# Dilated attention of a three-mixer encoder block: statistics and weights sent in other steps, the combination's small steps in PSUM, small jobs handed out every 2 products, another order at the end

## The chip, the cores and the metric

The kernel runs on one core of a Trainium2 chip. The metric is the device time of one execution in microseconds (us), as the median of several runs. One further execution was recorded by the hardware profiler; its own time and its span are given below. The core has five engines that run their own instruction streams and meet at semaphores: PE (TensorE, matmul, with weight loads shown apart as PEld), DVE (VectorE), ACT (ScalarE), POOL (GpSimd) and SP (SyncE, which here issues the DMAs, in order). Data is in SBUF (128 partitions), products come out in PSUM, which has 8 banks of 128 x 512 numbers in this kernel's use.

## The reference

One encoder block: a norm, one wide projection, three mixers side by side, a merge, an output projection, a norm and a residual. S = 1024 tokens, width D = 1024, each mixer 512 wide. The change is in the first mixer, dilated attention: 8 heads of 64, each computed in three groups (window, dilation) = (128, 1), (512, 4), (2048, 16), which are merged by a softmax over the groups' log-denominators.

```python
outs, lses = [], []
for gi, (window, dil) in enumerate(A_GROUPS):
    hs = slice(gi * A_HEADS, (gi + 1) * A_HEADS)
    o_g, lse_g = dilated_window_attention(aq[:, :, hs], ak[:, :, hs], av[:, :, hs], window, dil)
    outs.append(o_g)
    lses.append(lse_g)
wts = jax.nn.softmax(jnp.stack(lses, axis=0), axis=0)
oa = jnp.einsum('gbsh,gbshd->bshd', wts, jnp.stack(outs, axis=0)).reshape(b, s, BRANCH_WIDTH)
...
ya = (oa * jax.nn.silu(ga)) @ w_br_a
yb = (ob * jax.nn.silu(gb)) @ w_br_b
ym = (om * jax.nn.silu(gm)) @ w_br_m
merged = gates[:, :, 0] * ya + gates[:, :, 1] * yb + gates[:, :, 2] * ym
x = x + rms_norm(merged @ w_out, g_post)
```

## The kernel before

**Where the change lies.** The kernel runs its stages one after the other. In each, one or two kinds of work that use little PE are woven between long products that use nothing else, so that PE always has something to do. The last but one stage is the dilated attention, woven with the first 16 of the 24 branch projections (8 column tiles for each of 3 branches, the branch of this mixer last, since its operand is only then ready). The last stage (PSUM phase `ps_o`, function `y_part`) computes the rest of the projections and the output projection.

**Precision.** Operands of the big products are split into a high part (rounded, by ACT) and a low part (the difference, by DVE or POOL); each product is three matmuls: high x high, high x low, low x high. `wh` is the tile of a projection's split weights, `hh` and `hl` the two parts of this mixer's merged output, `bh` and `bl` those of the second mixer's.

**The products.** `add_y` queues projection m = 0 to 15: two halves of 512 tokens, each 12 matmuls (line 1880) into one of two PSUM banks `d`. What belongs to them, but isn't a matmul, is put on the list `pend`: the load of the weights of m + 2 (`y_load`, tile wr), the split of those of m + 1 (`y_split`: ACT line 1357, POOL line 1358), the load of the merge gate of m + 1 (`th_load`, tile wl), and the evacuation of each half (`y_evac`: DVE line 1378 multiplies in the bank, DVE line 1380 adds it to `acc`, which frees the bank). `weave` takes one job from `pend` after every third matmul. The products of m = 16, 17 and 18 have their weights split ahead too (17 and 18 into attention tiles that are free by then, `ak` and `aq`).

**The attention.** There are 12 items, (pair of heads p_, group g), g fastest. `plan` runs an item in four visits b and, after each, two steps T = 2b and 2b + 1 (`rest`). A visit computes scores (lines 1580, 1587), mask and exponential (1599 DVE, 1600 ACT), transposes the probabilities (1611, 1626, 1635, with DVE's copy to SBUF in 1639, tile `app`) and multiplies values with them (1652, 1659); the second half of an item overlaps with the first half of the next. `stats`, in visit 1 of the next item, transposes the minima and denominators, copies them (ACT) and writes them to `std` in DRAM (lines 1683 to 1690).

**The combination.** When all three groups of a pair are done, `ready` puts the 14 steps of `combine` on `todo`: fetch the statistics of the three groups, `shares` and `weights` (small DVE and ACT steps on 128 x 16 and 128 x 48 numbers, lines 1789 to 1803), `put` the weights to DRAM (`wgd`), `load` them spread over partitions (tile `wgt`, a ring of two), multiply the group's output (`weigh`, POOL line 1815), add (POOL line 1813), multiply with the SiLU gate (POOL line 1818, the gate itself in the `wgt` ring as well), and store or keep. `STEP_T` holds the step T of the current item in which each of the 14 is issued. Since `wgt` has two buffers, the load of group 2 waits for the multiply of group 0 and the gate's load for that of group 1.

**The last pair.** For p_ = 3 nothing is left to hide a trip through DRAM, so its weights are made otherwise: `rows` loads the statistics of groups 0 and 1 at T = 2 and T = 6 of the last item, `shares_3` turns them (line 1918) and computes weights in PSUM, `wide` (line 1952) spreads them with a matmul into banks W3B, and `first_two` and `third` (lines 1958 to 1966) combine the groups in halves of 512 tokens. `dl_high` (ACT, line 1858) and `dl_low` (line 1861) split the result, on DVE for the last pair.

**Order.** Each engine runs its instructions as issued, save that attention pieces are issued at a raised priority; `weave` moves to the next attention piece when the share of attention cost spent falls behind the share of product cost spent, so the costs given to the pieces decide where in the row of products each piece falls. DMAs go out on SP in order, those waiting for a buffer too.

Of the kernel before, what the change touches and what calls it, by code (L numbers as in the profile page):

```python
# [16 lines left out]
NT = 8  # L17
P = 128
# [32 lines left out]
def block(ctx: ExitStack, tc: tile.TileContext, x, xT, memT, cst, msk, bcst, tabA, gpost,  # L51
# [15 lines left out]
    def phase_psum(name, s2=0, s1=0, t=0, o=0):  # L67
        assert 2 * s2 + s1 + t + o <= 6
        bank["n"] = (s2, s1, t, o)
        bank["pool"] = tc.tile_pool(name=name, bufs=1, space=bass.MemoryType.PSUM, reuse_waits="tile")  # L70
        bank["p"] = bank["pool"].__enter__()
# [10 lines left out]
    def pst():  # L82
        return bank["p"].tile([P, 4, 128], F32, name="tr", tag="t", bufs=bank["n"][2])
# [90 lines left out]
    pend = []  # L174

    def weave(count, att=None, att_cost=0.0, lead=1.0, prio=ATT_PRIO):
        dg = run_items(count)
        dc = cost_items(count)
        d = a = 0.0
        steps = 0  # L180
        live_d, live_a = True, att is not None
        while live_d or live_a:
            if live_d and (not live_a or a / att_cost >= min(1.0, d / dc * lead)):
                try:
                    d += next(dg)
                    steps += 1
                    if pend and steps % 3 == 0:
                        pend.pop(0)()
                except StopIteration:
                    live_d = False  # L190
                    d = 1e18
            else:
                try:
                    with tc.high_priority(offset=prio):
                        a += next(att)
                except StopIteration:
                    live_a = False
# [1288 lines left out]
    with ExitStack():  # L1486
# [26 lines left out]
        def item(p_, g):  # L1513
# [155 lines left out]
            def stats():  # L1669
# [4 lines left out]
                if g == 0:  # L1674
                    A.activation(sr.rearrange("p (b a) -> p b a", b=16), tp[0:32, 0, :].rearrange("p (a b) -> p b a", b=16), AF.Copy)
                elif g == 1:
                    A.activation(sr.rearrange("p (b a) -> p b a", b=4), tp[0:32, 0, :].rearrange("p (a b) -> p b a", b=4), AF.Copy)
                else:
                    A.activation(sr, tp[0:32, 0, :], AF.Copy)
                dst = std[p_, g].rearrange("s h x -> (s h) x")  # L1680
# [14 lines left out]
                values=values, scores=scores, soft=soft, trans=trans, pv=pv, stats=stats)  # L1695

        def plan(it, pre, nxt):
# [7 lines left out]
            def tokens(T):  # L1705
# [11 lines left out]
                if n == 11:  # L1717
# [3 lines left out]
                    if T in (2, 6):  # L1721
                        j = T // 6
                        nc.sync.dma_start(rows[32 * j:32 * j + 32], std[3, j].rearrange("s h (t a) -> (s h t) a", t=NT))
# [5 lines left out]
            def visit(b):  # L1729
# [13 lines left out]
                if not it:  # L1743
                    shares_3(b)
                    return
# [7 lines left out]
            def rest(T):  # L1753
                combining(T)
                tokens(T)

            for b in range(4):
                out.append((lambda b=b: visit(b), SOFT + 100.0 if it else LAST_PAD))
                if it:
                    out += [(lambda T=T: rest(T), 0.5 * SOFT + 50.0) for T in (2 * b, 2 * b + 1)]  # L1760
# [9 lines left out]
        def combine(p_, ogs):  # L1770
# [15 lines left out]
            def shares():  # L1786
                cpt = c["t"]
                mn = cb.tile([P, 16], F32, name="cmn", bufs=2)
                V.tensor_tensor(mn, cpt[:, 0, 0], cpt[:, 1, 0], op=OP.min)
                V.tensor_tensor(mn, mn, cpt[:, 2, 0], op=OP.min)  # L1790
                c["e"] = eg = cb.tile([P, 3, 16], F32, name="ceg", bufs=1)
# [3 lines left out]
            def weights():  # L1795
                cpt, eg = c["t"], c["e"]
                dn = cb.tile([P, 3, 16], F32, name="cdn", bufs=1)
                V.tensor_tensor(dn, eg, cpt[:, :, 1], op=OP.mult)
                ds_ = cb.tile([P, 16], F32, name="cds", bufs=2)
                V.tensor_tensor(ds_, dn[:, 0], dn[:, 1], op=OP.add)  # L1800
                V.tensor_tensor(ds_, ds_, dn[:, 2], op=OP.add)
                V.reciprocal(ds_, ds_)
                V.scalar_tensor_tensor(eg, eg, 0.5, ds_[:, None, :].to_broadcast([P, 3, 16]), op0=OP.mult, op1=OP.mult)

            def put():
                for h in range(2):
                    E.dma_start(wgd[p_, h].rearrange("g (i e) -> i g e", e=16), c["e"][h * 64:h * 64 + 64])
# [26 lines left out]
        STEP_T = (4, 0, 1, 1, 2, 5, 6, 7, 7, 0, 3, 4, 5, 7)  # L1834
# [25 lines left out]
        def dl_low(k, t=slice(0, S)):  # L1860
            (V if k == 3 else G).tensor_tensor(hl[k][:, t], DL[k][:, t], hh[k][:, t].bitcast(F32), op=OP.subtract)
# [88 lines left out]
        def wide(g, x):  # L1950
            W3B[g, x] = pst().rearrange("p a b -> p (a b)") if g == 2 or x else pss1()
            PE.matmul(W3B[g, x], spread[:, g].rearrange("p h q -> p (h q)"), C["w"][0:96, half[x]], start=True, stop=True)

        def first_two(x):
            t = half[x]
            a, b = C["ogs"]
            for g, z in enumerate((a, b)):
                V.tensor_tensor(z[:, t], W3B[g, x], z[:, t], op=OP.mult)
            V.tensor_tensor(a[:, t], a[:, t], b[:, t], op=OP.add)

        def third(x):
            t = half[x]
            a, b = C["ogs"][0], OG[3, 2]
            V.tensor_tensor(b[:, t], W3B[2, x], b[:, t], op=OP.mult)
            V.tensor_tensor(a[:, t], a[:, t], b[:, t], op=OP.add)
            V.tensor_tensor(a[:, t], a[:, t], DL["g"][:, t], op=OP.mult)

        def ending():
# [3 lines left out]
                    (lambda: [third(0), dl_high(3, lo)], 2500.0)]  # L1972
# [8 lines left out]
        weave(16, every(), FIRST_PAD + 12 * NT * (SOFT + 100.0) + 4 * LAST_PAD + 10500.0)  # L1981
# [4 lines left out]
        third(1)  # L1986
        dl_high(3, hi)
        dl_low(3, lo)
        dl_low(3, hi)
# [344 lines left out]
```

## Time and profile before

| | us |
|---|---|
| median of 3 runs | 1414.26 |
| lowest, highest run | 1413.9, 1415.91 |
| the profiled execution | 1412.71 |
| its span, first to last instruction | 1410.9 |
| PE busy in it | 1379.7 |
| POOL busy in it | 574.7 |

The profile has a page (busy time of each engine, the chain of work that ended last, groups of instructions) and views of the trace: waits (who waited, for what, us in total, times, longest), windows (busy time of each engine in a stretch) and a timeline (start in us from the span's start, duration in us, engine, line of the kernel, operation, output<-input, shapes, and how many such instructions in a row the line stands for). A bracket at the end of a timeline row gives idle time of that engine just before and the event that ended it. In `PE d L1880 <- POOL wh L1358`, PE waited before writing d in line 1880 for POOL's writing of wh in line 1358. PE's matmuls overlap each other, so a matmul that shows 0.4 us starts well under 0.4 us after the one before.

### The profile page before, as it was taken

The numbers are of one execution on the slowest core, as the hardware profiler recorded it, in microseconds if no ns is written. First come the engines' busy times: TensorE is split into PE (matmuls) and PEld (weight loads), VectorE is DVE, ScalarE is ACT, GpSimd is POOL, SyncE is SP. The second block draws the span as 40 slices with busy tenths as digits, with TensorE's granted clock in tenths as the row PEclk, the third lists the DMA queues.
The fourth block names the chain that finished last, engine by engine and source line by source line (L and its number), as shares of the span: only waits on it lengthen the run. The fifth ranks groups of instructions, "written<-read, shape, count | busy, mean of one in ns | idle before, by whom it ended". The sixth has DMA issues, their size and how long they took to land.

```text
span 1410.9 us, 21845 instructions
## 1 busy us (share of the span) xinstructions
PE 1379.7 (98%) x7775; PEld 1106.2 (78%) x7775; DVE 1025.7 (73%) x1828; ACT 658.5 (47%) x1384; POOL 574.7 (41%) x440
## 2 busy tenths in 40 slices
PE   7999999999999999999999999999999999989997
PEld 7799986666655789988888888888887777767886
DVE  7768677767776597776877776677776557568977
ACT  6544355666555345333333333333345666653332
POOL 0507702675766000244555554455541153461003
PEclk9999999999999999999999999999999999999999
DMA  6355522322243688424332333333345676765455
GB/s 230 105 179 209 187 107 88 109 89 72 83 139 120 218 258 257 130 83 149 96 95 96 111 119 109 116 105 120 119 146 209 198 223 203 248 168 198 146 201 179
DMA packets 121933, 212.30 MB, mean 150 GB/s; under 512 B 32512, under 2 KB 61024, under 8 KB 121824
## 3 DMA queue, kind: packets, MB, share of 16 engines
q1 hardware_dynamic: 112512, 196.98, 43.0%
q10 hardware_dynamic: 9312, 13.93, 2.7%
q8 instruction: 61, 1.00, 0.3%
q14 instruction: 48, 0.39, 0.1%
HBM read 144.48 MB, written 66.38 MB: 149 GB/s over the span
## 4 chain that ended last, share of the span: by engine, by line
PE 87%; DVE 4%; POOL 3%; ACT 2%; issue 2%; DMA 1%; SPq 0%; DVEq 0%; POOLq 0%; ACTq 0%
PE s L1324 34%; PE d L1880 5%; PE s L1234 4%; PE s L2103 4%; PE ov L819 4%; PE sc L2021 3%; PE s L1285 3%; PE d L145 3%; PE d L147 3%; PE d L143 3%; PE s L1587 2%; PE s L804 2%; PE tr L1659 2%; PE s L803 2%; PE tr L785 2%
## 5 line engine op out<-in xcount | busy, mean ns | idle before, releaser
L810 POOL TENSOR_TENSOR bl<-bl,bp 128x512 f32<-128x512 f32 x96 | 132.7, 1382 | 54.2 <-ACT bp L806 48.7
L1324 PE MATMUL s<-hh,vS 128*128 128x512 f32 x400 | 133.4, 395 | 0.0
L1324 PE MATMUL s<-vA,vS 128*128 128x512 f32 x450 | 106.6, 390 | 0.0
L1599 DVE CUSTOM_DVE_ANT_0 pra<-s,mask 128x192 f32<-128x192 f32 (+2 forms) x192 | 52.7, 326 | 69.3 <-PE s L1587 34.7
L106 DVE TENSOR_TENSOR vS<-vot,vS 128x512 fp32r<-128x512 f32 x75 | 86.3, 1152 | 19.9 <-ACT vS L105 19.9
L1324 PEld LDWEIGHTS s<-vA,vS 128*128 128x128 f32 x450 | 84.5, 188 | 18.3
L806 ACT ACTIVATE bp<-s 128x512 f32<-128x512 f32 x128 | 75.6, 595 | 46.0 <-PE s L804 45.2
L786 DVE TENSOR_REDUCE bn<-tr 128x1 f32<-128x512 f32 x128 | 84.6, 683 | 11.0 <-PE tr L785 10.0
L1600 ACT ACTIVATE pra<-pra,sts 128x192 f32<-128x192 f32 (+2 forms) x176 | 75.2, 429 | 35.6 <-DVE sts L1599 35.3
L143 PE MATMUL d<-hh,wh 128*128 128x512 f32 x224 | 89.3, 399 | 1.3 <-DVE fth L216 1.3
L147 PE MATMUL d<-hh,wl 128*128 128x512 f32 x224 | 89.4, 399 | 0.0
L1324 PEld LDWEIGHTS s<-hh,vS 128*128 128x128 f32 x400 | 75.3, 188 | 17.7
L145 PE MATMUL d<-hl,wh 128*128 128x512 f32 x224 | 88.9, 397 | 0.0
L1324 PE MATMUL s<-hl,vS 128*128 128x512 f32 x200 | 79.1, 395 | 0.0
L1324 PE MATMUL s<-hh,wh 128*128 128x512 f32 x200 | 78.4, 392 | 0.0
L1324 PE MATMUL s<-hh,wl 128*128 128x512 f32 x200 | 78.4, 392 | 0.0
L1324 PE MATMUL s<-hl,wh 128*128 128x512 f32 x200 | 77.8, 389 | 0.0
L1328 ACT ACTIVATE vv<-s 128x512 f32<-128x512 f32 x50 | 29.9, 598 | 85.8 <-PE s L1324 59.2
L1068 POOL TENSOR_TENSOR vot<-wr 128x512 f32<-128x512 f32 x13 | 22.2, 1707 | 111.5 <-DVE wl L106 111.5
L819 PE MATMUL ov<-bp,VS 128*64 128x512 f32 x256 | 58.5, 598 | 0.0
L1068 POOL TENSOR_TENSOR vot<-vot,vA 128x512 f32<-128x512 f32 x12 | 19.3, 1608 | 90.8 <-DVE vS L106 90.8
L143 PEld LDWEIGHTS d<-hh,wh 128*128 128x128 f32 x224 | 42.2, 188 | 14.9 <-issue 5.5
(628 smaller groups left out, 4056.3 us busy)
## 6 DMA issues: line engine op xcount, KB each, us to landing
wr<-in_wu SPq DMA_DIRECT2D x40, 512.0 KB
vA<-in_wu SPq DMA_DIRECT2D x24, 512.0 KB
qkd<-ko SPq DMA_DIRECT2D x96, 128.0 KB
wl<-thd SPq DMA_DIRECT2D x24, 512.0 KB
wos<-os SPq DMA_DIRECT2D x12, 512.0 KB
wr<-in_wbr SPq DMA_DIRECT2D x24, 256.0 KB
aq<-qkd SPq DMA_DIRECT2D x12, 512.0 KB
ak<-qkd SPq DMA_DIRECT2D x12, 512.0 KB
```

What stands on the lines that cost most here:

```text
L106: V.tensor_tensor(dst_l, src, dst_h.bitcast(F32), op=OP.subtract)
L143: PE.matmul(dst, wh[:, k, :], hh[k][:, t], start=k == 0, stop=False)
L145: PE.matmul(dst, wh[:, k, :], hl[k][:, t], start=False, stop=False)
L147: PE.matmul(dst, wl[:, k, :], hh[k][:, t], start=False, stop=k == 7)
L786: fp["last"] = V.tensor_reduce(st[i]["n"][:, j, c:c + 1], s, axis=AX.X, op=OP.min)
L806: A.activation(pp, s, AF.Exp, scale=-1.0)
L810: G.tensor_tensor(lsum[i % 2], lsum[i % 2], pp, op=OP.add)
L819: PE.matmul(o[e * 64:e * 64 + 64], VS[:, kt, kv], d.pop(kt), start=kt < 2, stop=kt >= NT - 2)
L1234: PE.matmul(now[j], a, b, start=k == 0 and q == 0, stop=k == 3 and q == 2)
L1324: PE.matmul(BANK[n, c], a, b, start=k == 0 and q == 0 and not more, stop=k == 3 and q == 2, skip_group_check=c in "XW")
L1600: A.activation(src, src, AF.Exp, scale=-1.0, bias=bias, accum_out=sts[:, 1, h, T:T + 1])
L1880: PE.matmul(ps_, a, b, start=k == 0 and q == 0, stop=k == 3 and q == 2)
```

## The change

It has five parts.

1. The transfers of an item's statistics leave `stats` and become `send`, in step T = 3 of the next item (before: in visit 1). The second `rows` load of the last pair goes from T = 6 to T = 5.
2. `STEP_T`: most of the 14 steps of the combination are issued one step T later, `put` and the loads of groups 0 and 1 in steps of their own, and the load of group 2 in T = 0 of the next item.
3. `shares` and `weights` work in a PSUM bank: a copy and two minima, difference, exponential, product with the denominators and their sum (one reduction in place of two additions); only the reciprocal and the finished weights are in SBUF.
4. In this stage a job from `pend` is taken after every second matmul.
5. The end: `shares_3` becomes pieces of its own; `first_two` and `third` write their products back into the banks; the last half of `third` is a piece of the weave where it stood after it; the gate of the last pair and its low part go from DVE to POOL, in halves; `wide` skips banks of the ring `t` until group 2 gets the third and fourth of it; the attention's total cost in `weave` goes from 10500 to 13000 beyond the visits.

```diff
@@ -67,6 +67,7 @@
     def phase_psum(name, s2=0, s1=0, t=0, o=0):
         assert 2 * s2 + s1 + t + o <= 6
         bank["n"] = (s2, s1, t, o)
+        bank["i"] = 0
         bank["pool"] = tc.tile_pool(name=name, bufs=1, space=bass.MemoryType.PSUM, reuse_waits="tile")
         bank["p"] = bank["pool"].__enter__()
 
@@ -80,6 +81,7 @@
         return bank["p"].tile([P, 512], F32, name="s1", tag="s1", bufs=bank["n"][1])
 
     def pst():
+        bank["i"] += 1
         return bank["p"].tile([P, 4, 128], F32, name="tr", tag="t", bufs=bank["n"][2])
 
     def pso():
@@ -171,7 +173,7 @@
     def cost_items(count):
         return sum(q[2] for q in queue[done[0]:done[0] + count])
 
-    pend = []
+    pend, pace = [], [3]
 
     def weave(count, att=None, att_cost=0.0, lead=1.0, prio=ATT_PRIO):
         dg = run_items(count)
@@ -184,7 +186,7 @@
                 try:
                     d += next(dg)
                     steps += 1
-                    if pend and steps % 3 == 0:
+                    if pend and steps % pace[0] == 0:
                         pend.pop(0)()
                 except StopIteration:
                     live_d = False
@@ -1677,6 +1679,10 @@
                     A.activation(sr.rearrange("p (b a) -> p b a", b=4), tp[0:32, 0, :].rearrange("p (a b) -> p b a", b=4), AF.Copy)
                 else:
                     A.activation(sr, tp[0:32, 0, :], AF.Copy)
+                d["sr"] = sr
+
+            def send():
+                sr = d["sr"]
                 dst = std[p_, g].rearrange("s h x -> (s h) x")
                 if g == 0:
                     for z in range(4):
@@ -1692,7 +1698,7 @@
             return dict(
                 key=(p_, g),
                 ahead=seq[p_ * 3 + g + 2] if p_ * 3 + g + 2 < len(seq) else None,
-                values=values, scores=scores, soft=soft, trans=trans, pv=pv, stats=stats)
+                values=values, scores=scores, soft=soft, trans=trans, pv=pv, stats=stats, send=send)
 
         def plan(it, pre, nxt):
 
@@ -1718,8 +1724,8 @@
                     if T == 6:
                         DL["g"] = cb.tile([P, S], F32, name="wgt", bufs=2)
                         nc.sync.dma_start(DL["g"], g2d[0, 3])
-                    if T in (2, 6):
-                        j = T // 6
+                    if T in (2, 5):
+                        j = T // 5
                         nc.sync.dma_start(rows[32 * j:32 * j + 32], std[3, j].rearrange("s h (t a) -> (s h t) a", t=NT))
 
             def ready():
@@ -1741,7 +1747,6 @@
                 if b == 1 and pre and it:
                     pre["stats"]()
                 if not it:
-                    shares_3(b)
                     return
                 if b in (0, 2):
                     it["values"](b // 2)
@@ -1751,12 +1756,16 @@
                     qk_fetch(*it["ahead"])
 
             def rest(T):
+                if T == 3 and pre:
+                    pre["send"]()
                 combining(T)
                 tokens(T)
 
             for b in range(4):
-                out.append((lambda b=b: visit(b), SOFT + 100.0 if it else LAST_PAD))
-                if it:
+                out.append((lambda b=b: visit(b), SOFT + 100.0 if it else 0.5 * LAST_PAD))
+                if not it:
+                    out.append((lambda b=b: shares_3(b), 0.5 * LAST_PAD))
+                else:
                     out += [(lambda T=T: rest(T), 0.5 * SOFT + 50.0) for T in (2 * b, 2 * b + 1)]
             return out
 
@@ -1785,26 +1794,28 @@
 
             def shares():
                 cpt = c["t"]
-                mn = cb.tile([P, 16], F32, name="cmn", bufs=2)
-                V.tensor_tensor(mn, cpt[:, 0, 0], cpt[:, 1, 0], op=OP.min)
-                V.tensor_tensor(mn, mn, cpt[:, 2, 0], op=OP.min)
-                c["e"] = eg = cb.tile([P, 3, 16], F32, name="ceg", bufs=1)
+                b = pst().rearrange("p a b -> p (a b)")
+                mn = b[:, 0:16]
+                c["e"] = eg = b[:, 16:64].rearrange("p (g x) -> p g x", g=3)
+                c["n"] = b[:, 64:112].rearrange("p (g x) -> p g x", g=3)
+                V.tensor_copy(mn, cpt[:, 0, 0])
+                for g in (1, 2):
+                    V.tensor_tensor(mn, mn, cpt[:, g, 0], op=OP.min)
                 V.tensor_tensor(eg, cpt[:, :, 0], mn[:, None, :].to_broadcast([P, 3, 16]), op=OP.subtract)
                 A.activation(eg, eg, AF.Exp, scale=-1.0)
 
             def weights():
-                cpt, eg = c["t"], c["e"]
-                dn = cb.tile([P, 3, 16], F32, name="cdn", bufs=1)
+                cpt, eg, dn = c["t"], c["e"], c["n"]
                 V.tensor_tensor(dn, eg, cpt[:, :, 1], op=OP.mult)
                 ds_ = cb.tile([P, 16], F32, name="cds", bufs=2)
-                V.tensor_tensor(ds_, dn[:, 0], dn[:, 1], op=OP.add)
-                V.tensor_tensor(ds_, ds_, dn[:, 2], op=OP.add)
+                V.tensor_reduce(ds_, dn.rearrange("p g x -> p x g"), axis=AX.X, op=OP.add)
                 V.reciprocal(ds_, ds_)
-                V.scalar_tensor_tensor(eg, eg, 0.5, ds_[:, None, :].to_broadcast([P, 3, 16]), op0=OP.mult, op1=OP.mult)
+                c["w"] = w = cb.tile([P, 3, 16], F32, name="ceg", bufs=1)
+                V.scalar_tensor_tensor(w, eg, 0.5, ds_[:, None, :].to_broadcast([P, 3, 16]), op0=OP.mult, op1=OP.mult)
 
             def put():
                 for h in range(2):
-                    E.dma_start(wgd[p_, h].rearrange("g (i e) -> i g e", e=16), c["e"][h * 64:h * 64 + 64])
+                    E.dma_start(wgd[p_, h].rearrange("g (i e) -> i g e", e=16), c["w"][h * 64:h * 64 + 64])
 
             def weigh(g, add=False):
                 wv = wgt[g].rearrange("p (b a) -> p a b", b=16)
@@ -1831,7 +1842,7 @@
                     lambda: weigh(1, True), lambda: load(2), load_gate, lambda: weigh(2), lambda: weigh(2, True), gate, store]
 
         todo = []
-        STEP_T = (4, 0, 1, 1, 2, 5, 6, 7, 7, 0, 3, 4, 5, 7)
+        STEP_T = (5, 0, 1, 2, 3, 6, 7, 0, 0, 1, 4, 5, 6, 7)
         seq = [(p_, g) for p_ in range(4) for g in range(3)]
         items = [item(*x) for x in seq] + [None]
 
@@ -1858,7 +1869,7 @@
             A.activation(hh[k][:, t], DL[k][:, t], AF.Copy)
 
         def dl_low(k, t=slice(0, S)):
-            (V if k == 3 else G).tensor_tensor(hl[k][:, t], DL[k][:, t], hh[k][:, t].bitcast(F32), op=OP.subtract)
+            G.tensor_tensor(hl[k][:, t], DL[k][:, t], hh[k][:, t].bitcast(F32), op=OP.subtract)
 
         def add_y(m):
             n, i, f = steps[m]
@@ -1948,28 +1959,32 @@
                 dl_low(2)
 
         def wide(g, x):
+            while g == 2 and bank["i"] % 4 != 2 + x:
+                pst()
             W3B[g, x] = pst().rearrange("p a b -> p (a b)") if g == 2 or x else pss1()
             PE.matmul(W3B[g, x], spread[:, g].rearrange("p h q -> p (h q)"), C["w"][0:96, half[x]], start=True, stop=True)
 
         def first_two(x):
             t = half[x]
             a, b = C["ogs"]
-            for g, z in enumerate((a, b)):
-                V.tensor_tensor(z[:, t], W3B[g, x], z[:, t], op=OP.mult)
-            V.tensor_tensor(a[:, t], a[:, t], b[:, t], op=OP.add)
+            V.tensor_tensor(W3B[0, x], W3B[0, x], a[:, t], op=OP.mult)
+            V.tensor_tensor(a[:, t], W3B[1, x], b[:, t], op=OP.mult)
+            V.tensor_tensor(a[:, t], W3B[0, x], a[:, t], op=OP.add)
 
         def third(x):
             t = half[x]
             a, b = C["ogs"][0], OG[3, 2]
-            V.tensor_tensor(b[:, t], W3B[2, x], b[:, t], op=OP.mult)
-            V.tensor_tensor(a[:, t], a[:, t], b[:, t], op=OP.add)
-            V.tensor_tensor(a[:, t], a[:, t], DL["g"][:, t], op=OP.mult)
+            V.tensor_tensor(W3B[2, x], W3B[2, x], b[:, t], op=OP.mult)
+            V.tensor_tensor(a[:, t], W3B[2, x], a[:, t], op=OP.add)
+            G.tensor_tensor(a[:, t], a[:, t], DL["g"][:, t], op=OP.mult)
+            dl_high(3, t)
+            dl_low(3, t)
 
         def ending():
             DL[3] = C["ogs"][0]
             return [(lambda: [wide(g, 0) for g in range(2)], 500.0), (lambda: [wide(g, 1) for g in range(2)], 500.0),
                     (lambda: [first_two(0), wide(2, 0)], 2500.0), (lambda: [first_two(1), wide(2, 1)], 2500.0),
-                    (lambda: [third(0), dl_high(3, lo)], 2500.0)]
+                    (lambda: third(0), 2500.0), (lambda: third(1), 2500.0)]
 
         def every():
             yield from first()
@@ -1978,15 +1993,12 @@
             yield from run(plan(None, items[-2], None))
             yield from run(ending())
 
-        weave(16, every(), FIRST_PAD + 12 * NT * (SOFT + 100.0) + 4 * LAST_PAD + 10500.0)
+        pace[0] = 2
+        weave(16, every(), FIRST_PAD + 12 * NT * (SOFT + 100.0) + 4 * LAST_PAD + 13000.0)
         while pend:
             pend.pop(0)()
         y_split(18, V, qk.tile([P, S], R, name="aq", bufs=2))
         y_load(19)
-        third(1)
-        dl_high(3, hi)
-        dl_low(3, lo)
-        dl_low(3, hi)
         out_pool()
         for nm in ("B11", "B21"):
             for k in range(4):
```

## The prediction

> **What bounds the kernel now.** I read the page first: engines, then the chain by engine.
>
> ```profile
> span 1410.9 us, 21845 instructions
> PE 1379.7 (98%) x7775; PEld 1106.2 (78%) x7775; DVE 1025.7 (73%) x1828; ACT 658.5 (47%) x1384; POOL 574.7 (41%) x440
> PE 87%; DVE 4%; POOL 3%; ACT 2%; issue 2%; DMA 1%; SPq 0%; DVEq 0%; POOLq 0%; ACTq 0%
> ```
>
> TensorE is busy 98% of the span and carries 87% of the chain. The diff neither adds nor removes a product, so only stalls of PE in the edited stage (1065 to 1286 us) can be won or lost. That sends me to the waits, PE alone, in that window (us in total, times, longest):
>
> ```profile
> PE sc L2021 <- DVE og L1964: 2.7, 1, 2.7
> PE d L1880 <- DMA wgt<-wgd: 2.2, 1, 2.2
> PE tr L1659 <- DVE app L1639: 1.7, 1, 1.7
> ...
> ```
>
> Single stalls, each from another cause; with three shorter ones, shown below, they are a to f in order of time. A view of windows of pure products gives the unit: 46 in 10 us, a pitch of 0.22 us; a stall costs the distance of two starts less 0.22. The columns are busy us (and instructions) of PE, PEld, DVE, ACT, POOL, then granted clock, DMA share, GB/s; the first three rows are used later.
>
> ```profile
> 1154.00:1156.00 2.00, 2.00 (x34) 1.73 (x32) 0.20 (x1) 0.02 (x1) 2.00 (x2) 1.00 1.09 290
> 1204.00:1206.00 2.00, 2.00 (x30) 2.00 (x28) 0.00 (x0) 0.00 (x0) 1.54 (x1) 0.66 1.09 303
> 1206.00:1208.00 2.00, 2.00 (x25) 1.50 (x22) 0.64 (x9) 1.40 (x4) 1.92 (x2) 0.50 0.90 304
> 1310.00:1320.00 10.00, 10.00 (x46) 8.27 (x45) 9.38 (x13) 5.48 (x11) 0.00 (x0) 1.00 0.41 126
> ```
>
> The rest comes from the timeline: start, duration, engine, work, and in brackets idle time and its releaser.
>
> **The change part by part.** *Stalls a and b, the small halves of the weights (`y_split` on POOL, tile wh) behind a combining step.*
>
> ```profile
> 1157.51 0.40 PE L1880 MATMUL d<-hl,wh 128*128 128x512 f32 x1
> 1158.16 0.73 PE L1880 MATMUL d<-hh,wh 128*128 128x512 f32 x2 [0.25 <-POOL wh L1358]
> ...
> 1193.70 5.85 POOL L1815 TENSOR_TENSOR og<-og,wgt 128x1024 f32<-128x1024 f32 x2 [15.49 <-DMA wgt<-wgd]
> 1199.62 2.38 POOL L1813 TENSOR_TENSOR og<-og 128x1024 f32<-128x1024 f32 x1
> 1200.72 0.40 PE L1880 MATMUL d<-bl,wh 128*128 128x512 f32 x1
> 1201.96 1.26 POOL L1358 TENSOR_TENSOR wh<-wr,wh 128x512 fp32r<-128x512 f32 x1
> 1203.28 0.51 PE L1880 MATMUL d<-bh,wh 128*128 128x512 f32 x1 [2.15 <-DMA wgt<-wgd]
> ```
>
> The waits view names a DMA for b, but PE started 0.06 us after POOL's split ended (1201.96 + 1.26): POOL did two multiplies and an add in a row and the split stood behind the add. Pace 2 (the deferred small jobs handed out every 2 products in place of 3) and the shifted steps put both splits ahead of that 2.38 us add. Each becomes 2.38 us early against waits of 0.65 - 0.22 = 0.4 (a) and 2.56 - 0.22 = 2.3 (b): both go. After b the granted clock was 0.66 and 0.50 in two windows of 2 us, worth 0.34 x 2 + 0.50 x 2 = 1.7 more. a and b: 0.4 + 2.3 + 1.7 = 4.4.
>
> [...]
>
> *Stall c, the small steps of `combine`.*
>
> ```profile
> 1183.90 0.21 DVE L1803 SCALAR_TENSOR_TENSOR ceg<-ceg,cds 128x48 f32<-128x48 f32 x1
> ...
> 1234.33 2.38 POOL L1861 TENSOR_TENSOR hl<-hl,hh 128x1024 fp32r<-128x1024 f32 x1 [8.77 <-DMA avp<-vdr]
> 1234.39 2.38 DVE L1803 SCALAR_TENSOR_TENSOR ceg<-ceg,cds 128x48 f32<-128x48 f32 x1
> 1235.77 1.09 PE L1659 MATMUL tr<-app,avs 128*64 128x128 f32 x16
> 1238.54 0.90 PE L1659 MATMUL tr<-app,avs 128*64 128x128 f32 x12 [1.68 <-DVE app L1639]
> ```
>
> The same 128x48 instruction took 0.21 us once and 2.38 us here, where it began 0.06 us behind a POOL instruction and ended with it. Both its inputs lay in SBUF; PE then waited 1.7 us for the copy of probabilities queued behind it. In the changed kernel one input of each such step is in PSUM, so I price it at 0.21. But at this place pace 2 puts the two instructions of one evacuation (0.68 each, the L1380 row below) ahead of and inside the chain; about half of that is beyond the slack, so 0.65 of the wait stays. Gain 1.7 - 0.65 = 1.05 (bounds: 0.3 if both instructions count whole, 1.7 if none).
>
> *Stall d, evacuation of y products.*
>
> ```profile
> 1249.86 0.40 PE L1880 MATMUL d<-bh,wh 128*128 128x512 f32 x1
> 1250.37 0.68 DVE L1380 TENSOR_TENSOR acc<-d,acc 128x512 f32<-128x512 f32 x1
> 1251.20 0.47 PE L1880 MATMUL d<-bh,wh 128*128 128x512 f32 x1 [0.95 <-DVE acc L1380]
> ```
>
> PE waited for a bank whose add was popped too late: 1.34 - 0.22 = 1.1. Two evacuations of two halves handed out every 2 products instead of 3 come, by the order of the two programs, some 6 products (1.3 us) sooner; d goes whole.
>
> *Stall e, statistics of the last pair.*
>
> ```profile
> 1259.75 0.38 SPq L1723 DMA_DIRECT2D rows<-std  x1
> ...
> 1262.73 0.44 PE L1611 MATMUL tr<-cs,pra 128*128 128x128 f32 x2
> 1264.18 0.24 PE L1918 MATMUL s<-cs,rows 64*128 64x64 f32 x1 [1.01 <-issue]
> ```
>
> L1918 needs the second `rows` load, issued after the wl and g2d transfers; it is the only thing ready for PE. In the changed kernel it is issued at T=5, ahead of both, so sooner by the time that issuing them takes, and its packets don't follow 512 KB of theirs. 1.45 us between the starts less the second small transpose: 1.2 gained (bounds 0.5, 1.2). `send`, the std transfers one step later, delays nothing on this path: fetch waits for the last group's, and STEP_T moves fetch from T=4 to T=5 with it.
>
> *Stall f, the end.*
>
> ```profile
> 1281.41 0.39 PE L2021 MATMUL sc<-hh,wh 128*128 128x512 f32 x1
> 1283.10 0.68 DVE L1358 TENSOR_TENSOR aq<-wr,aq 128x512 fp32r<-128x512 f32 x1
> 1283.69 0.69 DVE L1964 TENSOR_TENSOR og<-tr,og 128x512 f32<-128x512 f32 x1
> 1284.52 0.47 PE L2021 MATMUL sc<-hh,ak 128*128 128x512 f32 x1 [2.72 <-DVE og L1964]
> ```
>
> The product pair m=17 takes the bank that `third(1)` (L1964) was reading, and this stood after 4 evacuation instructions and a split on DVE: 3.11 - 0.22 = 2.9. The change puts `third(1)` into the weave, aligns the bank so that m=17 needs only `first_two(1)` (about 2 us ahead of PE in my walk through the new order), and m=18 `third(1)`. It goes whole. The new price: the gates and small halves go to POOL in halves (1.26 each, the L1358 row above), and the split of aq waits, on ACT behind hh and on DVE beside POOL's last half. Walking the order with these durations, aq ends 0.9 us after PE needs it for its third product. Bounds 0 and 2.5 (two POOL halves in front).
>
> [...]
>
> *Load(2) after the next item's value loads.*
>
> ```profile
> 1149.98 1.26 SPq L1779 DMA_DIRECT2D wgt<-wgd  x2
> 1151.34 1.82 SPq L1529 DMA_DIRECT2D avs<-vdr  x2
> ...
> 1159.62 2.92 POOL L1815 TENSOR_TENSOR og<-og,wgt 128x1024 f32<-128x1024 f32 x1 [1.52 <-DMA wgt<-wgd]
> ...
> 1169.75 1.27 POOL L1358 TENSOR_TENSOR wh<-wr,wh 128x512 fp32r<-128x512 f32 x1
> 1171.47 0.39 PE L1880 MATMUL d<-bl,wh 128*128 128x512 f32 x1
> ```
>
> This is the one part that can lose much. POOL works in order, and the third multiply waited for this load (1159.62 - 1149.98 = 9.6 us from issue); the next split of the weights stands 11.4 us of POOL work behind it and finished 0.45 us before PE used it. Now load(2) comes on SP behind avs (1.82 us of issuing) and wl (512 KB, which the first window above moves in 1.8 us at 290 GB/s), which used to come after it. I take 2.0 later, between either alone and both (3.6): the split ends at 1173.0, PE needs it at 1171.5 - 0.4 (stall a gone) + 1.0 (pairs of products fall some 4 products later beside the attention) = 1172.1. Cost 1.0, bounds 0 and 2.6 (load 3.6 later), with the 1.7 of clock possible on top. At pair 1 the same chain has 4 us in hand:
>
> ```profile
> 1212.46 1.27 POOL L1358 TENSOR_TENSOR wh<-wr,wh 128x512 fp32r<-128x512 f32 x1 [0.20 <-ACT wh L1357]
> 1217.75 0.40 PE L1880 MATMUL d<-bl,wh 128*128 128x512 f32 x1
> ```
>
> *At nothing:* the other steps of `combine`, each one T later: POOL's wait for load(0), 15.49 us above, is empty time with nothing behind it that PE uses soon, and the results go to operands read after the weave. `send`: the same transfers, and SP no longer stands before sr when the queue has other loads to issue (a gain of which I count nothing). copy, reduction and exponential in PSUM (one DVE instruction fewer for each pair; about 0.2 us each, as L1803 above, and covered by products at all places but c); `shares_3` as pieces of its own (same work, same DVE queue).
>
> **Sum.** Gains 4.4 + 1.05 + 1.1 + 1.2 + 2.9 = 10.65; costs 1.0 + 0.9 = 1.9; net 8.75. The profiled execution took 1412.71 us (span 1410.9 and 1.8 around it): 1404.0 for it. The median of the runs, 1414.26, is 1.55 above that execution, so 1405.5 beside the median.
>
> **The rivals.**
> 1. *Half of it.* Load(2) comes 4 to 5 us later, the chain on POOL stalls PE at pair 0 (4.5 - 1.0 = 3.5 and 1.7 of clock) and c stays whole (1.05): net 10.65 - 1.05 - 0.9 - 5.2 = 3.5, so 1410.8. For it: POOL already waited 1.52 for that load with DMA share at 1.09. Against: avs and wl together are under 3 us of that rate.
> 2. *Slower.* Load(2) comes X late and stops both pairs' chains: (X - 1.0) at pair 0, (X - 4.0) at pair 1, and twice 1.7 of clock, against 10.65 - 0.9 = 9.75. From X = 5.7 the kernel isn't faster, from 7.1 it is slower by over 0.2%; at X = 8 it is 1414.26 - 9.75 + 4 + 7 + 3.4 = 1418.9. For it: 15.49 us of POOL's waiting on the earlier load. Against: the load would take 17.6 us where it took 9.6.
> 3. *It doesn't do what it says.* The stalls were not from the queues I name but from whatever is last behind them: an earlier split waits for its own load (wr), a bank freed earlier waits for its weights. Then each 2 us removed comes back at the next product: 1414.3. Against: in b, d and f the releaser ended within 0.15 us of PE's start.
>
> **How the numbers follow.** Forecast 0.62, rival 1 0.18, rival 3 0.08, rival 2 0.12. About 0.2% (2.8 us) is what a measurement of this kernel can tell from no change: faster means under 1411.4, slower over 1417.1. Faster: 0.62 and, of rival 1, 0.14: 0.76. Slower: 0.11 of rival 2. Within: 0.13. The forecast's own bounds: gains from 9.2 (c and e low) to 11.3, costs from 0 to 6.8: 1403 to 1411.9. The range runs from 1401, for queues that give more than I walked through, to 1412.5, where rival 1's upper half ends.
>
> **What would show it.** Right: no wait of PE over 0.7 us at wh, acc, rows or og; granted clock at 1.00 from 1200 to 1210; every L1803 at about 0.2 us (its successor in PSUM); m=17 starting straight behind m=16. Wrong: a new wait of PE for wh near 1172 or 1217, with POOL idle before its third multiply on wgt<-wgd; a wait for aq over 2.5 us near 1285; a low granted clock after either.

## The result and the profile after

| | us |
|---|---|
| before, median of 6 runs (lowest, highest) | 1414.43 (1413.9, 1415.91) |
| changed, median of 6 runs (lowest, highest) | 1408.0 (1406.78, 1410.23) |
| ratio to before, 95% interval | 0.9954 (0.9941 to 0.9967) |
| changed, the profiled execution (span) | 1409.11 (1407.3) |

The changed kernel is 6.4 us faster where 8.8 were forecast (1414.26 to 1405.5). Its waits of PE in the stage, read as before (us in total, times, longest):

```profile
PE d L1891 <- POOL wh L1360: 3.8, 1, 3.8
PE sc L2033 <- DVE aq L1360: 0.7, 1, 0.7
PE tr L1661 <- DVE app L1641: 0.3, 1, 0.3
PE tr L1654 <- DVE app L1615: 0.2, 1, 0.2
```

Line numbers have moved: 1891 is the product that was 1880, 1360 the split that was 1358. None of the six waits of before is left at its old size: no acc, no rows, no og, and the copy behind the small steps is down from 1.7 to 0.3. One wait is new and larger than any before. The timeline around it, from the load of group 2 for pair 0 on:

```profile
1148.79 2.57 SPq L1531 DMA_DIRECT2D avs<-vdr  x2
...
1151.45 0.57 SPq L1367 DMA_DIRECT2D wl<-thd  x1
...
1152.12 1.10 SPq L1788 DMA_DIRECT2D wgt<-wgd  x2
...
1163.55 2.94 POOL L1826 TENSOR_TENSOR og<-og,wgt 128x1024 f32<-128x1024 f32 x1 [6.90 <-DMA wgt<-wgd]
...
1170.75 0.40 PE L1891 MATMUL d<-bl,wh 128*128 128x512 f32 x1
...
1173.65 1.27 POOL L1360 TENSOR_TENSOR wh<-wr,wh 128x512 fp32r<-128x512 f32 x1
...
1174.97 0.80 PE L1891 MATMUL d<-bh,wh 128*128 128x512 f32 x1 [3.82 <-POOL wh L1360]
```

SP issues the two value loads and wl, and only then wgt. The multiply on POOL waits 6.90 us for it (1.52 before), and the split of the weights of m = 8, which needs nothing of this load, stands behind it in POOL's queue. PE starts 0.05 us after the split ends. Windows of 2 us over the same place (busy us and instructions of PE, PEld, DVE, ACT, POOL; granted clock, DMA share, GB/s) show what the gap leaves behind:

```profile
1172.00:1174.00 2.00, 0.00 (x0) 0.00 (x0) 0.10 (x1) 0.00 (x0) 2.00 (x2) 0.80 0.91 285
1174.00:1176.00 2.00, 1.03 (x3) 0.59 (x5) 0.00 (x0) 0.00 (x0) 0.92 (x1) 0.50 0.91 295
1176.00:1178.00 2.00, 2.00 (x12) 1.71 (x11) 0.30 (x1) 0.00 (x0) 0.00 (x0) 0.50 0.78 215
1178.00:1180.00 2.00, 2.00 (x10) 1.90 (x9) 1.62 (x9) 1.83 (x7) 0.00 (x0) 0.50 0.12 12
```

At a granted clock of 0.50, PE is busy for 1.03 + 2.00 + 2.00 us: half of that, 2.5 us, is lost besides the 3.8. The six waits of before make 8.7 us, and 1.7 of clock: 10.4. Those of the changed kernel make 5.0 and 2.5: 7.5. The difference, 2.9, accounts for most of the 3.6 us between the two profiled spans (1410.9 and 1407.3). The medians lie further apart than these two executions: that of before took 1.7 us less than its median, that of the changed kernel 1.1 more than its own.

Of all runs behind the numbers in this document one is left out: 1942.57 us, of the kernel with the second load of rows at T = 6, with a mean granted clock of 0.655 where all others have 0.99 to 1.00.

### The profile page after: what moved, and what is told of

It reads as the page before. It is cut to its first block, busy times and chain, and to the rows that moved or that the text cites. A ratio compares the mean times of both kernels' runs of the same rounds, so it can differ in the third digit from the quotient of the medians.

```text
span 1407.3 us, 21847 instructions
## 1 busy us (share of the span) xinstructions
PE 1381.3 (98%) x7775; PEld 1108.0 (79%) x7775; DVE 1021.6 (73%) x1824; ACT 658.8 (47%) x1384; POOL 579.7 (41%) x444
## 4 chain that ended last, share of the span: by engine, by line
PE 88%; DVE 3%; POOL 2%; ACT 2%; DMA 2%; issue 1%; SPq 0%; DVEq 0%; POOLq 0%; ACTq 0%
PE s L1326 34%; PE d L1891 6%; PE s L1236 4%; PE s L2115 4%; PE ov L821 3%; PE d L147 3%; PE d L145 3%; PE d L149 3%; PE s L1287 3%; PE sc L2033 3%; PE s L1589 2%; PE tr L1661 2%; PE s L806 2%; PE s L805 2%; PE tr L787 2%; PE d L2115 2%
```

## The experiments

The kernels ran in three groups, each beside the kernel before on the same chip. Its medians there were 1413.74, 1414.92 and 1414.08, so a distance between medians of two groups is good to about 1.2 us; ratios are free of that. "T7" is the changed kernel with load(2) at T=7.

| kernel | median us | ratio to before | 95% interval |
|---|---|---|---|
| changed, again | 1407.41 | 0.9954 | 0.9938 to 0.997 |
| changed, load(2) at T=7 ("T7") | 1402.9 | 0.9923 | 0.9911 to 0.9936 |
| T7, again | 1402.61 | 0.9916 | 0.9898 to 0.9935 |
| changed, split of m = 8 on DVE | 1404.64 | 0.993 | 0.9913 to 0.9948 |
| changed, pace 3 | 1409.13 | 0.9971 | 0.9961 to 0.998 |
| changed, small steps in SBUF | 1411.21 | 0.9978 | 0.9967 to 0.9989 |
| changed, old end | 1407.05 | 0.9954 | 0.9938 to 0.997 |
| T7, old end | 1408.94 | 0.9963 | 0.9949 to 0.9977 |
| T7, pace 3 | 1409.89 | 0.9969 | 0.9958 to 0.998 |
| T7, rows at T=6 | 1407.95 | 0.9958 | 0.9944 to 0.9971 |
| T7, statistics sent in visit 1 | 1409.7 | 0.9973 | 0.9953 to 0.9993 |
| before, pace 2 alone | 1408.8 | 0.9966 | 0.9952 to 0.998 |

### Load(2) back at T=7

```diff
-lambda: weigh(1, True), lambda: load(2), load_gate,
+lambda: load(2), lambda: weigh(1, True), load_gate,
-STEP_T = (5, 0, 1, 2, 3, 6, 7, 0, 0, 1, 4, 5, 6, 7)
+STEP_T = (5, 0, 1, 2, 3, 6, 7, 7, 0, 1, 4, 5, 6, 7)
```

> The changed kernel with one step moved back: load(2) is issued at T=7, ahead of the next item's value loads, as before the change; nothing else differs, POOL's order is the same. In the changed kernel's profile the third multiply waited 6.90 us for that load and PE then waited 3.82 us for wh at 1171 us, with the granted clock at 0.50 until 1180 (2.5 us more). Theory (the place of load(2) costs the stall and the low clock behind it): both go, 6.3 us, median 1401.7 where the changed kernel has 1408.0, no wait of PE for wh. Rival (the DMA engines are full there and the load lands as late from either place, or the value loads pay for it): the third multiply starts within 1 us of where it did, or a wait for app or avs of 3 us takes its place; median 1407 to 1409.

The timeline has the load issued 3.6 us sooner and the multiply without any wait; the waits of PE in the stage are all that is left.

```profile
1148.53 1.10 SPq L1788 DMA_DIRECT2D wgt<-wgd  x2
...
1157.28 2.94 POOL L1826 TENSOR_TENSOR og<-og,wgt 128x1024 f32<-128x1024 f32 x1
```

```profile
PE sc L2033 <- DVE aq L1360: 0.7, 1, 0.7
PE tr L1661 <- DVE app L1641: 0.3, 1, 0.3
PE tr L1654 <- DMA avs<-vdr: 0.2, 1, 0.2
```

The multiply starts 6.3 us sooner, the wait for wh is gone, the granted clock is 1.00 in every window of 1 us from 1064 to 1296, and the value loads, now behind wgt, cost 0.2. The median of 1402.9 is 5.1 below the changed kernel's 1408.0 (1.2 short of the theory). The same file a second time:

> The kernel with load(2) at T=7 once more, beside the changed kernel. Theory: 5 to 6.3 us below the changed kernel, ratio to before 0.991 to 0.9935, no low clock anywhere in the stage. Rival (the first measurement was a lucky one): 1405 or more.

1402.61, 4.8 below the changed kernel beside it. Both rivals fall: the gain came again, and no wait of any size took the place of the removed one.

### The split of m = 8 on another engine

```diff
-pend.append(lambda: y_split(m + 1, G))
+pend.append(lambda: y_split(m + 1, V if m == 7 else G))
```

> The changed kernel, load(2) as late as it is there, with the small half of the weights of m = 8 made on DVE in place of POOL. Theory (what holds PE at 1171 us is the order of POOL's queue behind the late multiply, not the transfer as such): POOL still waits about 7 us for wgt, PE waits for no wh there, at most 0.9 us for bl (POOL ends it at 1173.7, PE needs it at about 1172.8); no low clock; median 1402 to 1404. Rival (the wait moves to bl or to DVE, whose split has two inputs in SBUF beside POOL's 2.9 us multiply): a wait of 2 us or more, 1405 to 1408.

Waits of PE, the two new ones:

```profile
PE tr L1661 <- DMA avs<-vdr: 1.4, 1, 1.4
...
PE s L1929 <- DMA rows<-std: 0.6, 1, 0.6
```

No wait for wh and none for bl. The load was late here too (POOL's third multiply waited 5.31 us for it, and 5.61 in the changed kernel run beside it), so it is the order of POOL's queue that passed the lateness on to PE. What the theory missed is a wait for values of 1.4 us, which comes in its place; the median, 1404.64, lies just above what was expected.

### The changed kernel again

> The changed kernel once more, as it is, beside the next three. [...] Rival (the low clock belongs to the place): 0.50 from 1173 to 1180 us again.

The profiled execution took 1404.76 us this time. Its wait for wh, and two windows after it:

```profile
PE d L1891 <- POOL wh L1360: 2.6, 1, 2.6
```

```profile
1172.00:1174.00 2.00, 1.28 (x11) 1.00 (x11) 0.00 (x0) 0.00 (x0) 0.67 (x1) 1.00 1.03 331
1174.00:1176.00 2.00, 2.00 (x17) 1.79 (x14) 1.69 (x9) 1.22 (x5) 0.00 (x0) 1.00 0.49 134
```

The wait is there again (2.6 us for 3.8) and the clock stays at 1.00, where it was 0.50: the low clock doesn't belong to the place. Ten runs spread over 1404.4 to 1414.46 us; the four of the T7 kernel beside them over 1401.81 to 1404.02.

### Pace 3

```diff
-pace[0] = 2
+pace[0] = 3
```

> The changed kernel with the small jobs taken after every third matmul as before; STEP_T, PSUM steps and ending as changed. Theory (pace 2 is what removed stalls a and d): the split of wh stands behind the 2.38 us add again at pair 0 and the bank's add is late again, 0.4 + 1.1 us back; the load of wl comes behind load(2), so the wait at 1171 us may shrink by about 1 us; median 1408 to 1410, and a wait of PE for acc of about 1 us in the profile. Rival (the shift of STEP_T alone removed them): no wait for acc, median 1407 or less.

```profile
PE d L1891 <- DVE acc L1382: 4.0, 4, 2.4
PE d L1891 <- POOL wh L1360: 1.5, 2, 1.3
```

The number came out, 1409.13, but as a balance: acc costs 4.0 us in four places and not 1, while the waits for wh shrink from 3.8 to 1.5, since wl now comes behind load(2), and the granted clock is 1.00 from 1064 to 1296. In the T7 kernel there is no such balance:

> The kernel with load(2) at T=7 (1402.9) and, in it, small jobs after every third matmul as before the change. Theory (pace 2 carries the evacuations in time; the other parts of the change make it more needed, not less): waits of PE for acc as in the changed kernel with pace 3, 4.0 us in four places, median 1407. Rival (those waits were pushed out by the late load(2)): 1403 to 1404.

The same 4.0 us for acc, in four places, and 1.7 of clock behind the longest (0.84 granted in the us from 1233, 0.50 in the next three, 0.95 in the fifth): 1409.89, 7.0 above the T7 kernel. That is 2.9 more than the 1407 expected; the low clock is part of it. Pace 2 is needed for the evacuations, and the late load(2) had no part in it.

### Pace 2 alone

```diff
-if pend and steps % 3 == 0:
+if pend and steps % pace[0] == 0:
...
+pace[0] = 2
 weave(16, every(), ...
```

> The kernel before with only the pace changed: small jobs of this stage after every second matmul. POOL's order then has the split of wh ahead of the 2.38 us add at pairs 0 and 1. Theory (pace 2 alone removes a, b with the low clock behind it, and d: 0.4 + 4.0 + 1.1): 1408.3 where before has 1413.7; c, e and the end remain as waits. Rival (the moved steps are needed for it): a wait for wh of over 2 us and a low clock remain, 1412 to 1414.

Waits of PE in the kernel before with this edit alone:

```profile
PE tr L1652 <- DMA avs<-vdr: 2.2, 3, 1.5
PE s L1918 <- issue: 1.7, 1, 1.7
PE d L1880 <- POOL wh L1358: 1.5, 1, 1.5
PE sc L2022 <- DVE og L1964: 0.4, 1, 0.4
```

1408.8 us, as forecast (1408.3), but not by the forecast's account. Stalls a, b and d are gone; so, unexpectedly, is c, and the end is down from 2.7 to 0.4. In exchange there are waits for values and for wh at pair 1, and e has grown from 1.0 to 1.7, with 1.7 of low clock behind it (granted 0.50 from 1262 to 1265, 0.82 in the next us). Why c is gone is seen on DVE and POOL: the small step ran clear of POOL's instruction but for its last 0.08 us.

```profile
1233.73 0.21 DVE L1803 SCALAR_TENSOR_TENSOR ceg<-ceg,cds 128x48 f32<-128x48 f32 x1
```

```profile
1233.86 2.39 POOL L1861 TENSOR_TENSOR hl<-hl,hh 128x1024 fp32r<-128x1024 f32 x1 [8.77 <-ACT hh L1858]
```

### The small steps back in SBUF

```diff
-                b = pst().rearrange("p a b -> p (a b)")
-                mn = b[:, 0:16]
+                mn = cb.tile([P, 16], F32, name="cmn", bufs=2)
...
-                V.scalar_tensor_tensor(w, eg, 0.5, ds_[:, None, :]...
+                V.scalar_tensor_tensor(eg, eg, 0.5, ds_[:, None, :]...
```

> The changed kernel with shares and weights in SBUF as before the change. Theory (PSUM operands are what keeps POOL's instructions from stretching them): one of the steps is stretched to over 1 us beside a POOL instruction again and PE waits for app, 1.0 to 2.0 us; median 1409 to 1410. Rival (in the changed kernel POOL's 2.38 us instruction starts at 1235.80 us, when the chain of small steps is all but done, so the shifted order alone avoids the meeting): all steps 0.2 us, median 1408.0 within 0.7.

```profile
1235.44 2.36 POOL L1870 TENSOR_TENSOR hl<-hl,hh 128x1024 fp32r<-128x1024 f32 x1 [5.74 <-ACT hh L1867]
```

```profile
1235.50 2.37 DVE L1812 SCALAR_TENSOR_TENSOR ceg<-ceg,cds 128x48 f32<-128x48 f32 x1
```

The one step of this chain that began behind POOL's instruction (by 0.06 us) took 2.37 us in place of 0.21 and ended with it; the seven before it took 0.17 to 0.25 each. PE then waited 2.5 us for the copy of app, with low clock behind it (granted 0.50 from 1241 to 1244, 0.84 in the next us). 1411.21: what the theory forecast came, at a larger price than it gave. In the changed kernel itself the same step, with one input in PSUM, starts 0.08 us ahead of POOL's instruction (1235.72 and 1235.80), so this one run can't tell PSUM from timing. The kernel with the split of m = 8 on DVE can: there the step starts 0.09 behind it.

```profile
1230.78 2.37 POOL L1872 TENSOR_TENSOR hl<-hl,hh 128x1024 fp32r<-128x1024 f32 x1 [5.94 <-ACT hh L1869]
```

```profile
1230.87 0.21 DVE L1814 SCALAR_TENSOR_TENSOR ceg<-tr,cds 128x48 f32<-128x48 f32 x1 [0.21 <-DMA ak<-qkd]
```

It takes 0.21 us all the same; the input in PSUM is what sets it apart from the 2.37. Pair 0 says so too. The product with the denominators took 0.92 us in SBUF beside a POOL split that began at 1134.38, and in the changed kernel, with one input in PSUM beside the split that began at 1134.37, 0.22.

### The old end

```diff
-(lambda: third(0), 2500.0), (lambda: third(1), 2500.0)]
+(lambda: [third(0), dl_high(3, lo)], 2500.0)]
...
-weave(16, every(), ... + 13000.0)
+weave(16, every(), ... + 10500.0)
...
+third(1)
+dl_high(3, hi)
+dl_low(3, lo)
+dl_low(3, hi)
```

(with `wide`, `first_two`, `third` as before, and the last low part on DVE)

> The changed kernel with wide, first_two, third and the splits of the last pair as before the change (the last third after the weave, gate and low part on DVE, no skipped banks, 10500 for the cost); shares_3 stays in pieces. Theory (the end was worth 2.9 less 0.7 us): PE waits 2.5 to 3 us for og in the last stage instead of 0.67 for aq; median 1410.2. Rival (the gain at the end came from the longer row of products left there, or comes out elsewhere): median 1408.0 within 0.7.

```profile
PE d L1891 <- POOL wh L1360: 3.9, 1, 3.9
PE sc L2033 <- DVE og L1975: 3.2, 1, 3.2
```

The wait for og is back at 3.2, yet the ratio is that of the changed kernel. The wait for wh has moved from pair 0 (1171 us) to pair 1 (1213 us), because the smaller total cost puts the products elsewhere beside the attention. With that wait in both kernels and in different places, this run doesn't price the end; its profiled execution, 1410.69 us, was also the slowest of its six. So the same end in the T7 kernel:

> The kernel with load(2) at T=7 (median 1402.9, ratio to before 0.9923) and, in it, the end as before the change (also 10500 for the cost). It asks again what the end is worth, without the wait for load(2), which in the first try with the old end fell at another place and may have hidden it. Theory (the wait of m=17 for the last third is worth 2.9 us, 0.7 of it given back to aq): PE waits 3 us for og and the median is 1405.3. Rival (the end is worth nothing): 1402.9 within 0.7.

```profile
PE sc L2033 <- DVE og L1975: 3.2, 1, 3.2
PE tr L1654 <- DMA avs<-vdr: 1.7, 2, 1.5
PE s L1929 <- DMA rows<-std: 0.5, 1, 0.5
```

1408.94, 6.0 above the T7 kernel, more than either theory gave: the wait for og as expected, 1.5 of low clock behind it (granted 0.67, 0.50 and 0.98 in windows of 2 us from 1278), and 2.2 us of waits for values and rows from the other alignment. The end with its cost is worth much; how much of it is the end alone, without the alignment, wasn't separated.

### The second load of rows at T=6

```diff
-if T in (2, 5):
-    j = T // 5
+if T in (2, 6):
+    j = T // 6
```

> The kernel with load(2) at T=7 (1402.9) and, in it, the second load of rows at T=6 as before the change. Theory (stall e was this load's place behind wl and the gate): PE waits about 1.2 us ahead of the transposes of rows, median 1404.1. Rival (send in T=3 and pace 2 alone removed it): 1402.9 within 0.7 and no wait there.

```profile
1253.93 0.37 SPq L1729 DMA_DIRECT2D rows<-std  x1
```

```profile
1258.99 0.34 PE L1929 MATMUL s<-cs,rows 64*128 64x64 f32 x1 [3.90 <-DMA rows<-std]
```

3.90 us where stall e was 1.01 in the same view, and low clock behind it (granted 0.50 from 1259 to 1262, 0.83 in the next us): 1407.95 (1407.36 to 1409.32), 5.0 above the T7 kernel. wl and the gate's load stand ahead of this load here, as they did before; the T7 kernel issues it 2.6 us sooner, at 1251.29. What has changed is when PE wants it: 1.2 us after its issue (from 1255.1 on), and 3.4 us in the kernel before. The place of this one load is worth more with the rest of the change than it cost without.

### The statistics sent in visit 1

```diff
                 if b == 1 and pre and it:
                     pre["stats"]()
+                    pre["send"]()
...
-                if T == 3 and pre:
-                    pre["send"]()
```

> The kernel with load(2) at T=7 (1402.9) and, in it, the statistics sent in visit 1 as before the change, not at T=3. Theory (send is worth nothing by itself): 1402.9 within 0.8. Rival (SP standing before sr holds the value loads and load(2)): a wait of PE for avs or wh of over 1 us, 1404.5 or more.

The theory falls: 1409.7, 7.1 above the T7 kernel beside it. PE waits for values in four places, and POOL's first multiply of pair 1 comes 4.1 us later than in the T7 kernel. First this kernel, its wait, its SP queue at pair 0 and its POOL at pair 1; then the T7 kernel's queue and POOL at the same places:

```profile
PE tr L1654 <- DMA avs<-vdr: 3.4, 4, 1.8
```

```profile
1137.53 1.39 SPq L1689 DMA_DIRECT2D std<-sr  x4
1139.01 1.25 SPq L1817 DMA_DIRECT2D wgd<-ceg  x2
...
1196.25 5.81 POOL L1825 TENSOR_TENSOR og<-og,wgt 128x1024 f32<-128x1024 f32 x2 [17.38 <-DMA wgt<-wgd]
```

```profile
1136.23 1.25 SPq L1818 DMA_DIRECT2D wgd<-ceg  x2
1138.62 1.39 SPq L1689 DMA_DIRECT2D std<-sr  x4
...
1192.17 2.89 POOL L1826 TENSOR_TENSOR og<-og,wgt 128x1024 f32<-128x1024 f32 x1 [15.04 <-DMA wgt<-wgd]
```

Sent early, the four std transfers stand ahead of the weights (wgd) on SP, and SP stands before them until ACT has written sr. At pair 0 the weights were ready on DVE at 1135.11 and sr at 1137.50. The weights leave 2.8 us later than in the T7 kernel; of this 0.8 reaches the loads (1140.90 for 1140.10) and 1.1 the first multiply (1146.69 for 1145.61) and load(2), which waits for that multiply. The value loads wait on SP behind load(2), and PE's first wait for them, 1.08 us at 1159.70, with another of 0.33 just behind it, leaves 1.7 us of low clock (granted 0.50 from 1162 to 1165, 0.81 in the next us). At pair 1 the weights leave 6.2 us later (1188.88 for 1182.65). The waits for values and this clock make 5.1 of the 7.1 us; the rest isn't seen in the profiled execution, the fastest of its seven.

## Why the prediction was right or wrong

**Right in direction, and in the mechanism of the gain.** Stalls a, b, d, e and f went whole, as forecast, and c to 0.3 (forecast 0.65 left). The aq price was forecast at 0.9 and is 0.7. Its rows in the changed kernel:

```profile
1282.20 1.30 POOL L1872 TENSOR_TENSOR hl<-og,hh 128x512 fp32r<-128x512 f32 x1 [0.74 <-ACT hh L1869]
...
1282.68 1.37 DVE L1360 TENSOR_TENSOR aq<-wr,aq 128x512 fp32r<-128x512 f32 x1 [1.89 <-ACT aq L1359]
```

The split with two inputs in SBUF took 1.37 us where it took 0.68 before, with POOL idle; it ends 0.55 after POOL's half does. Nearly all of PE's 0.7 us is this stretch of 0.69. When the change was priced, only the L1803 row (2.38 us) spoke for a DVE step held up by the POOL instruction beside it, and no row for one input in PSUM keeping such a step at 0.21; both prices were estimates. The runs show 1.37 and 2.37 us with two inputs in SBUF beside POOL, and 0.21 and 0.22 with one in PSUM.

**Mis-sized: load(2).** The mechanism was named, at its place and with the chain of 11.4 us behind it (it took 11.4 again, from 1163.55 to 1174.92). Its size was not: the load was to be 2.0 later, 3.6 at most. It was 3.9: 2.1 in issue (1152.12 for 1149.98) and 1.8 in flight (11.4 us for 9.6). PE needed the split at 1171.0 and not at 1172.1. Price 3.8 and 2.5 of clock in this execution, 2.6 and none in the other, against a forecast of 1.0 (bounds 0 and 2.6, with 1.7 of clock possible on top). This is the sign that the prediction named for being wrong: a wait for wh near 1172 us, POOL idle before its third multiply, a low clock behind it. The T7 kernel shows the term by itself: 5.1 and 4.8 us between medians. The term was some 4 us too small; the forecast was off by 2.4 only (8.8 for 6.4), so the other parts together gave some 1.6 more than was summed (T7 alone, without this term: 10.8 for 9.75). That the two errors lie on opposite sides is luck.

**Wrong: `send` at nothing.** The prediction named how it could gain, SP no longer standing before sr, and counted nothing for it. Without it the T7 kernel loses 7.1 us. The step asked whether the statistics' own path is delayed, and not what stands behind them on SP: the weights of the pair in hand.

**Wrong: the gains as a sum of parts.** Taken out of the T7 kernel one at a time, pace, end, rows and send cost 7.0, 6.0, 5.0 and 7.1, together 25.1 us (the first three up to 1.2 less each, as they were set against another group's median), where T7 gains 10.8 in all (1413.74 to 1402.9). Pace 2 alone gave 6.1 (1414.92 to 1408.8). The parts aren't additive: each holds a place in queues that the others shift, and a missing one shows as a new wait elsewhere, in all four profiles with low clock behind it (1.5 to 1.7 us). Stall e, put at 1.2, and stall c, credited to PSUM, are of this kind: pace 2 alone made e larger (1.7) and removed c.

**Rivals.** The first, half of it by the POOL chain at pair 0, names what happened at pair 0 (3.5 of wait and 1.7 of clock, measured 3.8 and 2.5), but c did not stay, and its sum (1410.8) is too high. The second (a late load(2) stopping two pairs) didn't come: at pair 1 POOL's multiply began at 1213.00, 8.6 later than before, and the split behind it ended at 1222.05, but PE had attention to do until 1222.33, its next product. It was near: with the old end that place took the 3.9 us wait. The third falls, as the removed waits show.

## What to carry to other kernels

On an engine or a queue that works in order, price a moved step by what stands behind it, and not by what it feeds: the late load cost because a split that had nothing to do with it waited behind its user, and early statistics cost because another pair's weights stood behind them on SP. When many small edits shift one common order, test the finished version by taking out one at a time; a sum of parts priced in the old order is only a start. Then look for the one new wait in the profile: moving one load back gave almost as much again as all the rest.

## What the runs showed of the hardware

**The clock fell behind some gaps of PE and not behind others, and each time for 3.4 us or twice that.** The kernel with the old end and the T7 kernel with the old end stop PE for the same 3.2 us, for the same reason, at the same point of the program. Windows at the end of the gap and behind it, first of the former, then of the latter (granted clock third from the right):

```profile
1280.00:1282.00 2.00, 0.00 (x0) 0.00 (x0) 1.97 (x4) 1.02 (x2) 0.00 (x0) 1.00 0.99 262
1282.00:1284.00 2.00, 1.48 (x7) 1.25 (x8) 1.93 (x4) 0.14 (x1) 0.00 (x0) 1.00 0.98 365
```

```profile
1278.00:1280.00 2.00, 1.47 (x4) 1.21 (x5) 1.93 (x4) 0.13 (x1) 0.00 (x0) 0.67 0.93 357
1280.00:1282.00 2.00, 2.00 (x7) 1.51 (x6) 1.91 (x4) 2.00 (x5) 0.00 (x0) 0.50 1.05 405
1282.00:1284.00 2.00, 2.00 (x10) 1.68 (x9) 2.00 (x4) 1.62 (x4) 0.00 (x0) 0.98 0.92 361
```

One stays at 1.00; in the other the missing clock adds up to (0.33 + 0.50 + 0.02) x 2 = 1.7 us, that is 3.4 us at half clock (PE was busy in all but 0.5 us of these windows). The stall b of before gives the same sum (0.34 + 0.50 in 2 us each: 3.4 us at half), and the 3.8 us gap of the changed kernel twice that, from 1173.2 to 1180.0. Over all profiles of this stage, in windows of 1 us, the missing clock adds up to 1.70 or 1.71 us behind eight gaps (the two waits of 1.08 and 0.33 counted as one), and to 3.42 and 3.41 behind two: the 3.8 us of the changed kernel and the 3.9 us of the one with the old end. Short gaps were enough: 2.3 us in the kernel before, 1.7 us with pace 2 alone, and the two waits of 1.08 and 0.33 us with the statistics sent early. Nor is a longer gap sure to cost it: the 2.6 us of the changed kernel's second profile left the clock at 1.00. The spread of the runs goes with the gaps: the changed kernel, with a gap of 3.8 and of 2.6 us in its two profiles, took 1404.4 to 1414.46, the T7 kernel, whose longest wait is 0.7, 1401.81 to 1404.02, and pace 2 alone, with waits of up to 1.7, 1406.15 to 1413.79. What decides which gap costs clock these runs don't show.
